# Storing the low halves of split projection weights once, and loading them in later groups

## The chip, the cores and the metric

The kernel runs on one core of one Trainium2 chip. The metric is the device time of one execution in microseconds; times of several executions are given as their median. The core has five engines that each work through a queue of their own in order: TensorE (PE, with its weight loads shown as PEld), VectorE (DVE), ScalarE (ACT), GpSimd (POOL) and SyncE (SP, which issues DMA transfers here; ACT and POOL issue some as well). An engine that waits for a semaphore holds back everything behind it in its queue.

## The reference

One layer of a residual block over 2048 tokens of width 1024, in float32. A normalised input goes through one wide projection, whose 5376 columns feed three consumers: chunk-band attention, an RWKV-7 recurrence, and two gates.

```python
h    = rms_norm(x, pre_mix_g)
proj = h @ w_in                       # (2048, 1024) @ (1024, 5376)
p_att, p_rwkv, p_gate = proj[:, :1536], proj[:, 1536:3328], proj[:, 3328:] + gate_bias
y_a  = chunk_band_attention(*split(p_att, 3), rel_bias)
y_b  = rwkv7_time_mix(p_rwkv, ...)
m    = sigmoid(gate_a) * (y_a @ proj_a) + sigmoid(gate_b) * (y_b @ proj_b)
x    = x + rms_norm(m @ w_out, post_mix_g)
x    = x + rms_norm(square(relu(rms_norm(x, pre_ffn_g) @ w_up)) @ w_down, post_ffn_g)
```

## The kernel before

The 2048 tokens are worked off in four groups of 512. Each group runs `phase_rwkv` (14 column blocks of the RWKV part, 16 of the gates, and the recurrence), `phase_attention` (12 column blocks, three for each of four head pairs: q, k, v) and `phase_merge` (the two branch projections and `w_out`, with the next group's normalisation beside them). The feed-forward part follows after all four groups.

A matmul in full float32 precision is made from three in a faster 32-bit format: every operand is split into a high part (a rounded copy) and a low part (what the rounding lost), and high times high, high times low and low times high are added up in PSUM. `split` (L80) makes the parts: ACT copies the high part (L81), DVE subtracts it from the raw values (L83). For weights, `wsplit` (L70) first has SP load the raw block of 128 by 1024 values, 512 KB (`load_raw`, L64), into a buffer `wraw`, and writes `whi` and `wlo`. Each of the three has two buffers, so the raw load for a block waits until the block two earlier has been split, and the parts of a block are written when the matmuls of the block two earlier have read theirs. The same buffers serve `proj_a`, `proj_b` and `w_out`.

`dense` (L118) makes one column block of 128 columns: it calls `wsplit` and then issues 24 matmuls of 128x512 (`mm3`, L86): eight of the high weight with the high input (`hh,whi` in the profile), eight of the high weight with the low input (`hl,whi`), and last the eight that read the low weight (`hh,wlo`). All 42 blocks (14 + 16 + 12) are made in each of the four groups, from the same weights, so each weight block is loaded and split four times. In the first group the first two blocks are loaded ahead (`self.raws`), and their low parts are made by POOL instead of DVE.

The order of each engine's queue comes from a scheduler that goes through the program with estimated times. Some places are fixed by hand: `queue_behind` puts one instruction behind another of the same engine, `follow` (L112) does it for the two split instructions of a block behind the instructions that emptied an earlier PSUM bank (`self.emptied`), and the constants `GATES`, `STEPS`, `BLOCKS`, `TURNED`, `FIFTH`, `BONUS`, `SCORES` and `TURNS` place small matmuls of the recurrence among the dense ones by number.

Other lines that are spoken of below: L399 and L400 (POOL copies the last column of a block for the token shift), L497 (POOL copies row scales `n`), L738 and L743 (matmul `ps_st` and DVE update `ST` of the recurrence), L713 and L716 (`TQ`), L770 to L784 (the recurrence's output, `yn`, stored as `yd` by POOL), L585 (`ps_A`), L926 and L927 (keys `KK` and values `VV` of the group before, loaded by SP), L960 and L961 (their stores by POOL), L988 to L1018 (attention scores `ps_s`, row minima `mn`, exponentials, `PT`, `ps_pv`), L1077 (the bias of a head, loaded by SP), L1149 (the branch projections, `th`), L1178 and L1189 (`ps_o`, `o`), L1200 and L1202 (the rows of the group before, loaded by SP for `residual`), L1231 and L1255 (`cmb`, `wd`: sums of `w_down` blocks, made beside the groups and moved by POOL).

Of the kernel before, what the change touches and what calls it, by code (L numbers as in the profile page):

```python
# [9 lines left out]
F32 = mybir.dt.float32  # L10
BF16 = mybir.dt.bfloat16
F32R = mybir.dt.float32r
# [4 lines left out]
DRAM = bass.MemoryType.DRAM  # L17

P = 128
D = 1024  # L20
KB = D // P
# [17 lines left out]
BONUS = {(0, 1): 138, (1, 0): 258}  # L39
SCORES = 150  # L40
TURNS = {1: (588, 592)}
DEC = math.exp(-0.5)

ATT0 = 0
# [12 lines left out]
class Block:  # L57
# [54 lines left out]
    def follow(self):  # L112

        for ins, done in zip((self.high.ins, self.low), self.emptied[-3] if len(self.emptied) > 2 else ()):
            if done is not None:
                self.queue_behind(ins, done.ins)

    def dense(self, col):  # L118

        first = bool(self.raws)  # L120
        wh, wl = self.wsplit(self.w_in(col), "w", KB, P, lower=self.nc.gpsimd if first else None)
        if first:
            n = 1 - len(self.raws)
            self.queue_behind(self.high.ins, self.highs[n])
        self.follow()
        ps = self.pd.tile([P, G], F32, tag="d", name="psd")
        terms = [(wh[:, k], wl[:, k], self.h[0][:, k], self.h[1][:, k]) for k in range(KB)]
        if first:
            pairs = [(u, h) for u, _, h, _ in terms] + [(v, h) for _, v, h, _ in terms] + [(u, l) for u, _, _, l in terms]
            self.mm = [  # L130
                self.nc.tensor.matmul(ps, l, r, start=n == 0, stop=n == len(pairs) - 1).ins
                for n, (l, r) in enumerate(pairs)
            ]
            self.queue_behind(self.mm[0], self.last_transpose)
        else:
            self.mm = self.mm3(ps, terms, True)
        self.dl += self.mm
        return ps
# [19 lines left out]
    def constants(self, ctx, mixing):  # L158
        tc, nc, a = self.tc, self.nc, self.a
        keep = ctx.enter_context(tc.tile_pool(name="const", bufs=1))  # L160
        cp = mixing.enter_context(tc.tile_pool(name="mconst", bufs=1, side="right"))
        dp = ctx.enter_context(tc.tile_pool(name="scratch", bufs=1, space=DRAM))
        nrow = sum(n for _, n in ROWS)
        self.cst = cp.tile([P, nrow], F32, name="cst")
        nc.sync.dma_start(self.cst, a["cst"])
# [279 lines left out]
    def rwkv_pre(self, g, p, rp, NA, between=lambda: None):  # L445
# [20 lines left out]
        between()  # L466
        nc.vector.tensor_scalar(tw, tw, -0.5 * DEC, -0.5 * DEC, ALU.mult, ALU.add)
        cum = tw
# [279 lines left out]
    def rwkv_post(self, p, R):  # L748
# [18 lines left out]
        for h in range(2):  # L767
            ps = self.pr.tile([C, 4, P], F32, tag="wus", name="ps_yt")
            for j in range(4):
                mm = nc.tensor.transpose(ps[:, j], yn[:, h * 4 + j], self.ident)  # L770
                if j == 0 and p in TURNS:
                    self.place(mm, TURNS[p][h])
            cs = slice(h * 4, h * 4 + 4)
# [876 lines left out]
```

## Time and profile before

| | |
|---|---|
| median of 3 executions | 3199.82 us (3198.31 to 3202.85) |
| profiled execution | 3198.07 us, of which the span from first to last instruction is 3196.4 us |
| PE busy | 3147.3 us, 98% of the span |
| DVE busy | 2235.8 us, 70% |
| ACT busy | 1578.7 us, 49% |
| POOL busy | 613.8 us, 19% |
| DMA | 598.82 MB, mean 187 GB/s |
| granted clock of TensorE | 0.999 |

How to read the profile's lines: a line of a group of instructions gives the kernel's line, the engine, the operation, output and inputs by the program's names, the shape, and the count after an x; behind the bar the busy time in us and the mean of one in ns; behind the second bar the idle time of the engine just before them and what ended most of it. A line of waits gives who waited, for whom, the total in us, how many times, and the longest. A line of the DMA issues gives the queue, the count, the size of one, and the median time from issue to landing. A line of the timeline gives start and length in us, the engine (SPq, POOLq: an engine's queue that waits or issues), the operation, and how many were merged. "issue" as a releaser means that the engine waited for nothing that the profile shows.

### The profile page before, as it was taken

Reading aid. Unit: us, or ns where it says so; the run is one execution under the profiler, and the core shown is the slowest. Engines: PE = TensorE matmul, PEld = TensorE weight load, DVE = VectorE, ACT = ScalarE, POOL = GpSimd, SP = SyncE. Lnnn points to the kernel's source line nnn. Section 1 sums busy time; section 2 is a strip of 40 time slices with the busy share of each in tenths; the row PEclk is TensorE's granted clock in tenths of the full one; section 3 lists DMA queues with packets and bytes.
Section 4 is the critical chain, followed back from the end, with each engine's and each line's share of the span. In section 5 each row is a group of like instructions: output and inputs, shape, how many; then the busy total and the mean of one; then the engine's idle time right before and its main releaser. Section 6 shows DMA issues by size and latency. Waiting matters only on the chain. (4 is left out here: it accounts for less than half of the span.)

```text
span 3196.4 us, 49803 instructions
## 1 busy us (share of the span) xinstructions
PE 3147.3 (98%) x18800; PEld 2575.3 (81%) x18800; DVE 2235.8 (70%) x3668; ACT 1578.7 (49%) x2511; POOL 613.8 (19%) x1119
## 2 busy tenths in 40 slices
PE   8999999999999999999999999999999999999998
PEld 6877788778888877888877888888888878888887
DVE  6785667776767786767876776877656768765564
ACT  5435645445745445745534755454544454444343
POOL 3222012132112222112222101221211112210000
PEclk9999999999999999999999999999999999999999
DMA  6245473157573246574236466554877866547565
GB/s 192 86 135 189 134 259 129 60 172 244 175 260 129 77 141 245 186 235 160 94 116 228 160 208 261 192 179 162 293 268 251 281 225 213 170 156 244 191 221 174
DMA packets 197477, 598.82 MB, mean 187 GB/s; under 512 B 25570, under 2 KB 25708, under 8 KB 197236
## 3 DMA queue, kind: packets, MB, share of 16 engines
q1 hardware_dynamic: 139124, 415.24, 40.1%
q0 software_dynamic: 48896, 163.61, 13.6%
q10 hardware_dynamic: 9216, 16.78, 1.4%
q8 instruction: 148, 2.42, 0.3%
q14 instruction: 93, 0.76, 0.1%
HBM read 431.67 MB, written 167.01 MB: 187 GB/s over the span
## 5 line engine op out<-in xcount | busy, mean ns | idle before, releaser
L1469 PE MATMUL ps_dn<-fop 128*128 128x512 f32 x2688 | 610.8, 389 | 0.0
L1469 PEld LDWEIGHTS ps_dn<-fop 128*128 128x128 f32 x2688 | 504.1, 188 | 104.7 <-DVE fop L83 0.2
L81 ACT CAST whi<-wraw 128x1024 fp32r<-128x1024 f32 x232 | 243.5, 1049 | 284.4 <-PE psd L92 202.5
L83 DVE TENSOR_TENSOR wlo<-wraw,whi 128x1024 fp32r<-128x1024 f32 x230 | 280.6, 1220 | 125.4 <-ACT whi L81 80.2
L92 PE MATMUL psd<-hh,whi 128*128 128x512 f32 x1328 | 357.9, 398 | 1.1 <-ACT k L401 1.0
L92 PE MATMUL psd<-hh,wlo 128*128 128x512 f32 x1328 | 356.8, 398 | 0.0
L92 PE MATMUL psd<-hl,whi 128*128 128x512 f32 x1328 | 354.3, 397 | 0.0
L92 PEld LDWEIGHTS psd<-hl,whi 128*128 128x128 f32 x1328 | 243.6, 188 | 47.9
L92 PEld LDWEIGHTS psd<-hh,wlo 128*128 128x128 f32 x1328 | 242.7, 188 | 48.3
L92 PEld LDWEIGHTS psd<-hh,whi 128*128 128x128 f32 x1328 | 241.2, 188 | 50.0 <-ACT k L401 1.6
L83 DVE TENSOR_TENSOR fop<-xraw,fop 128x1024 fp32r<-128x1024 f32 x112 | 137.0, 1223 | 176.2 <-ACT fop L81 175.8
L81 ACT CAST fop<-xraw 128x1024 fp32r<-128x1024 f32 x112 | 117.8, 1052 | 251.0 <-PE ps_dn L1469 191.9
L1339 POOL DMA_DIRECT2D xd<-X x192 | 104.1, 542 | 380.3 <-ACT X L1336 318.2
L83 DVE TENSOR_TENSOR fop<-wdraw,fop 128x1024 fp32r<-128x1024 f32 x112 | 136.6, 1219 | 19.7 <-ACT fop L81 19.4
L81 ACT CAST fop<-wdraw 128x1024 fp32r<-128x1024 f32 x112 | 117.6, 1050 | 35.7 <-DMA wdraw<-in_w_down_dram 22.7
L994 DVE CUSTOM_DVE_ANT_0 sc<-bias,ps_s 128x640 f32<-128x640 f32 (+4 forms) x128 | 93.8, 733 | 39.3 <-PE ps_s L988 23.3
L1012 DVE TENSOR_TENSOR PTl<-ps_pt,PTh 128x640 fp32r<-128x640 f32 (+4 forms) x128 | 94.3, 737 | 27.7 <-ACT PTh L1011 26.8
L1001 ACT ACTIVATE sc<-sc,mn 128x640 f32<-128x640 f32 (+4 forms) x128 | 97.8, 764 | 31.8 <-DVE mn L994 30.4
L81 ACT CAST s12h<-s 128x1024 fp32r<-128x1024 f32 x32 | 33.7, 1053 | 155.5 <-PE ps_u L92 155.5
L92 PE MATMUL ps_p<-yh,whi 128*128 128x512 f32 x256 | 101.7, 400 | 4.9 <-DVE th L1149 2.2
L92 PE MATMUL ps_p<-yl,whi 128*128 128x512 f32 x256 | 101.5, 397 | 0.3 <-DVE yl L83 0.2
L1178 PE MATMUL ps_o<-whi,mh 128*128 128x512 f32 x256 | 100.5, 392 | 0.7 <-DVE o L1189 0.6
(374 smaller groups left out, 6804.0 us busy)
## 6 DMA issues: line engine op xcount, KB each, us to landing
wraw<-in_w_in_dram SPq DMA_DIRECT2D x168, 512.0 KB, 3.7
xraw<-xd SPq DMA_DIRECT2D x112, 512.0 KB, 4.5
xd<-X POOLq DMA_DIRECT2D x192, 256.0 KB, 4.7
wraw<-in_w_up_dram SPq DMA_DIRECT2D x80, 512.0 KB, 4.4
wdraw<-wd SPq DMA_DIRECT2D x64, 512.0 KB, 4.8
wdraw<-in_w_down_dram SPq DMA_DIRECT2D x48, 512.0 KB, 5.0
gd<-gate ACTq DMA_DIRECT2D x64, 256.0 KB, 2.5
wd<-cmb POOLq DMA_DIRECT2D x64, 256.0 KB, 3.7
```

Of the source, the lines that this page charges most:

```text
L81: high = self.high = self.nc.scalar.copy(hi, src)
L83: self.low = lower.tensor_tensor(lo, src, hi.bitcast(F32), ALU.subtract).ins
L92: mm.append(nc.tensor.matmul(ps, l, r, start=n == 0, stop=n == last).ins)
L994: least = nc.vector.tensor_tensor_reduce(sc[:, 0:n], bias[:, s0:640], pss[:, c0 : c0 + n], 1.0, 3.0e38, ALU.add, ALU.min, mn,)
L1001: nc.scalar.activation(sc[:, 0:n], sc[:, 0:n], AF.Exp, scale=-1.0, bias=mn, accum_out=sm[:, col : col + 1])
L1012: nc.vector.tensor_tensor(lv, pst[:, 0:nk], hv.bitcast(F32), ALU.subtract)
L1178: nc.tensor.matmul(ps[t], l[:, k, ts], r[:, k % 2], start=k == 0 and j == 0, stop=k == KB - 1 and j == 2)
L1339: nc.gpsimd.dma_start(self.xd[q][i // 2][:, i % 2], src)
L1469: nc.tensor.matmul(ps, o[:, l, k, sl], o[:, r, k], start=start and n == 0, stop=stop and n == end)
```

## The change

In the first group, the low part of every block is made as before and is then also stored to a DRAM scratch tile of 512 KB of its own (`wlow`, 42 of them) by a DMA that POOL issues. In the other three groups, `dense` loads the raw block as before and has ACT make the high part as before, but there is no subtraction: SP loads the low part from DRAM straight into the `wlo` buffer. `follow` has then only the ACT copy to put behind something. `LOWS` lists the blocks by number; it holds all 42. The matmuls and their order in the program are the same.

```diff
+LOWS = range(42)
...
     def follow(self):
 
         for ins, done in zip((self.high.ins, self.low), self.emptied[-3] if len(self.emptied) > 2 else ()):
-            if done is not None:
+            if done is not None and ins is not None:
                 self.queue_behind(ins, done.ins)
 
     def dense(self, col):
 
         first = bool(self.raws)
-        wh, wl = self.wsplit(self.w_in(col), "w", KB, P, lower=self.nc.gpsimd if first else None)
+        kept = self.lows.get(col)
+        if kept is None:
+            wh, wl = self.wsplit(self.w_in(col), "w", KB, P, lower=self.nc.gpsimd if first else None)
+            if col in self.keep_lows:
+                kept = self.lows[col] = self.dp.tile([P, KB, P], F32, name=f"wlow{col // P}")
+                self.nc.gpsimd.dma_start(kept, wl.bitcast(F32))
+        else:
+            raw = self.load_raw(self.w_in(col), KB, P)
+            wh, wl = (self.wp.tile([P, KB, P], F32R, tag="w" + x, bufs=2, name="w" + n) for x, n in (("h", "hi"), ("l", "lo")))
+            self.high = self.nc.scalar.copy(wh, raw)
+            self.low = None
+            self.nc.sync.dma_start(wl.bitcast(F32), kept)
...
-        dp = ctx.enter_context(tc.tile_pool(name="scratch", bufs=1, space=DRAM))
+        dp = self.dp = ctx.enter_context(tc.tile_pool(name="scratch", bufs=1, space=DRAM))
+        self.lows = {}
+        self.keep_lows = {i * P for i in LOWS}
```

## The prediction

> **What bounds the kernel now.** I read the table by engine first, then five stretches: the four groups (one pass each over 512 tokens, cut where the dense blocks of the next begin) and the feed-forward part.
>
> ```profile
> span 3196.4 us, 49803 instructions
> PE 3147.3 (98%) x18800; PEld 2575.3 (81%) x18800; DVE 2235.8 (70%) x3668; ACT 1578.7 (49%) x2511; POOL 613.8 (19%) x1119
> ...
> 0.00:483.00 483.00, 462.22 (x3149) 368.06 (x3150) 342.82 (x698) 241.25 (x448) 102.39 (x189) 1.00 0.50 164
> 483.00:976.00 493.00, 487.17 (x3417) 398.64 (x3416) 358.90 (x660) 255.47 (x442) 110.40 (x200) 1.00 0.51 172
> 976.00:1469.00 493.00, 488.21 (x3419) 399.00 (x3418) 359.44 (x661) 256.28 (x445) 109.51 (x201) 1.00 0.51 172
> 1469.00:1963.00 494.00, 488.45 (x3422) 400.01 (x3421) 357.10 (x651) 252.55 (x434) 101.12 (x184) 1.00 0.49 165
> 1963.00:3196.40 1233.40, 1221.24 (x5398) 1009.60 (x5396) 817.54 (x1001) 573.12 (x745) 190.42 (x347) 1.00 0.64 218
> ```
>
> A stretch lists its length, then busy time and count of PE, PEld, DVE, ACT and POOL, the clock, the DMA share and GB/s. In groups 1 to 3 PE is busy 487.17 to 488.45 us of 493 or 494, at full clock; DVE about 359. Those groups are the ones that the change relieves, and together they leave PE 493 + 493 + 494 - 487.17 - 488.21 - 488.45 = 16.2 us idle. Since "busy" may hide small gaps (matmuls overlap), I then asked what PE and its weight loads wait for, in these groups alone (first group of rows PE, second PEld):
>
> ```profile
> PE ps_st L738 <- DVE ST L743: 3.2, 3, 1.1
> PE ps_s L988 <- DVE mn L994: 2.4, 4, 0.7
> PE ps_p L92 <- DVE th L1149: 1.6, 3, 0.7
> PE ps_s L723 <- DVE TQ L716: 1.3, 3, 0.5
> PE ps_g L92 <- DVE yn L761: 1.2, 3, 0.4
> ...
> PE ps_o L1178 <- DVE wlo L83: 0.5, 1, 0.5
> PE ps_o L1178 <- DVE o L1189: 0.3, 1, 0.3
> PE ps_a L428 <- DVE BR L603: 0.2, 1, 0.2
> ...
> PEld ps_st L738 <- DVE ST L743: 12.5, 24, 1.5
> ...
> PEld ps_s L988 <- DVE mn L994: 9.7, 30, 1.0
> PEld ps_A L585 <- issue: 8.8, 24, 0.4
> ```
>
> The reader is to see how little is lost to DVE. All of PE's idle time that DVE ends is 3.2 + 2.4 + 1.6 + 1.3 + 1.2 + 0.5 + 0.3 + 0.2 = 10.7 us, in three groups. The weight loads show more, but the row of ps_A waits for nothing and yet costs 8.8 / 24 = 0.37 us each time: that is the price of the switch itself. Above it, ST leaves 12.5 - 24 x 0.37 = 3.6 us and mn (9.7 / 30 = 0.32 each) nothing on the mean.
>
> **The change part by part.** First, what one block costs and when it is needed.
>
> ```profile
> L83 DVE TENSOR_TENSOR wlo<-wraw,whi 128x1024 fp32r<-128x1024 f32 x230 | 280.6, 1220 | 125.4 <-ACT whi L81 80.2 <-PE psd L92 37.6 <-issue 6.8
> L92 PEld LDWEIGHTS psd<-hh,wlo 128*128 128x128 f32 x1328 | 242.7, 188 | 48.3
> ...
> 1028.54 1.23 DVE L83 TENSOR_TENSOR wlo<-wraw,whi 128x1024 fp32r<-128x1024 f32 x1 [1.00 <-PE psd L92]
> 1028.75 2.01 PE L92 MATMUL psd<-hh,whi 128*128 128x512 f32 x8
> 1030.60 1.98 PE L92 MATMUL psd<-hl,whi 128*128 128x512 f32 x8
> 1032.42 1.98 PE L92 MATMUL psd<-hh,wlo 128*128 128x512 f32 x8
> 1034.23 1.98 PE L92 MATMUL psd<-hh,whi 128*128 128x512 f32 x8
> ...
> wraw<-in_w_in_dram SPq DMA_DIRECT2D x168, 512.0 KB, 3.7
> kc<-KK POOLq DMA_DIRECT2D x12, 512.0 KB, 3.8
> KK<-kc SPq DMA_DIRECT2D x12, 512.0 KB, 4.8
> VV<-vc SPq DMA_DIRECT2D x12, 512.0 KB, 6.5
> ...
> 761.65 0.74 POOL L960 DMA_DIRECT2D kc<-KK  x1 [6.76 <-DVE KK L945]
> ```
>
> Removed: 3 x 42 = 126 subtractions x 1.220 = 153.7 us of DVE, 51 us a group, so about 359 falls to 308 of 493. Kept: 126 high copies on ACT, all matmuls. What is hidden behind PE is worth nothing; on the path lie at most the 10.7 us above, and below nothing cannot be excluded, as the order of the queues may come out worse. DVE sheds 51 / 359 = 14%. The rows name ST, mn and TQ, chains of their own that go on taking their time, and only one names wlo (0.5 us). I take 3 us gained of 10.7, nearer to the low end for that reason.
>
> Added: 126 loads of 512 KB on SP's queue, 66 MB in about 1480 us, 45 GB/s on top of 165 to 172, when the feed-forward stretch shows 218 with PE as busy. Each load waits until the last matmul of two blocks earlier has left the buffer (two buffers). From then to the third part of its own block, which reads the low part first, PE has to do one whole block (1034.23 - 1028.75 = 5.48 us) and two thirds of another (1032.42 - 1028.75 = 3.67), 9.1 us, less some 0.2 by which matmuls overlap. The load takes 3.7 to 6.5 us by the rows, so 2.4 us are left at the worst of them: hidden. If the cover goes (a landing over 9 us), PE waits for the rest, with nothing to make it up. Behind a waiting load stands SP's queue: later raw weights, bias, keys and values. But this queue waits today as well, for the subtraction of the block two earlier, which itself starts only when PE has left that buffer:
>
> ```profile
> SPq L67 <- DVE wlo L83: 956.9, 172, 36.4
> ...
> SPq L1077 <- DMA yd<-yf: 16.2, 3, 5.8
> ```
>
> So the new wait ends some 1.2 us sooner than the old one, and the raw loads, released by the ACT copy now, start earlier. Zero for these, with one exception in the rivals.
>
> Added in group 0: 42 stores issued by POOL, 0.74 us each by the kc row, 31 us on an engine that is busy 102 of 483, and 22 MB in those 483 us, 46 GB/s on top of 164, again within the 218. POOL waits for each subtraction and holds back what comes after it in its queue (the carry column of the token shift, the row scales n, cmb and wd traffic). The buffer is held until the store lands: 0.74 + 3.8 = 4.5 us after the subtraction, while the block that reads it starts only at 1034.23 in the steady rows and holds the buffer for 5.5 us more, to about 1039.7, against 1029.8 + 4.5 = 1034.3 for the store: some 5.4 us to spare. For more than that POOL must be late, and its longest wait of this kind in group 0 shows that it can be:
>
> ```profile
> POOL pr L399 <- DVE k L402: 15.5, 3, 12.3
> ```
>
> A store behind all of the 12.3 us would hold the subtraction of two blocks later back by 12.3 - 5.4 = 6.9 us, and what follows on DVE with it; the low part itself has 9.1 - 1.2 = 7.9 us to spare, so PE would not yet wait for it. Bounds: 0, and 6.9 if the work behind it on DVE is what PE needs next; I take 0.5, since one such wait is in the row and the next longest must fit in 15.5 - 12.3 = 3.2 us. The first two blocks are split on POOL itself, after the last operation that PE's start waits for, so nothing there. The feed-forward part is untouched.
>
> Sum against the profiled execution (3198.07 us, 1.7 over its span and 1.75 under the median of 3199.82): -3 + 0.5 = -2.5. To this I add 2 us for the exception below at less than full size. On the median that is 3199.82 - 0.5 = 3199.3, **3199 us**: no difference. About 0.2% (6.4 us) is what a measurement of this kernel can tell from no change.
>
> **The rivals.** *Slower: the v block of the first head pair waits for its low part.* At the start of attention in groups 1 to 3 SP's queue carries keys, values, the former group's rows and biases at once:
>
> ```profile
> 748.22 0.62 POOL L784 DMA_DIRECT2D yd<-yf  x1 [3.87 <-DVE yf L783]
> 749.35 7.15 SPq L1077 DMA_DIRECT2D bias<-skew  x2
> 750.56 1.98 PE L92 MATMUL psd<-hh,wlo 128*128 128x512 f32 x8
> 756.54 0.88 SPq L926 DMA_DIRECT2D KK<-kc  x1
> 757.47 0.60 SPq L927 DMA_DIRECT2D VV<-vc  x1
> 758.17 1.48 SPq L67 DMA_DIRECT2D wraw<-in_w_in_dram  x2
> 761.77 1.98 PE L92 MATMUL psd<-hh,wlo 128*128 128x512 f32 x8
> ```
>
> The second bias load stands until 756.2 for the landing of yd (the row L1077 <- yd above: three times, up to 5.8 us). The low part of the v block is free to load at 750.56 + 1.98 = 752.5 and needed at 761.77. Queued ahead of that bias it lands by 752.5 + 6.5 = 759.0, hidden. Queued behind bias, KK and VV it is issued at 758.1, lands by 764.6, and PE loses 2.8 us a group, 8.5 in all; if it takes as long as yd does in this burst (issued at 748.2, landed by 756.1: 7.9), it lands at 766.0, and PE loses 4.2 a group, 12.7 in all. It decides from 3.2 us a group on (9.5 less the 3 gained is 6.5). Which one is queued first the trace doesn't show; for the bad order speaks that KK and VV stand ahead of the raw weight that waits for just this block. With 3 gained and 0.5 lost in group 0: 3206 to 3210, 3208 in the middle. The Trainium skill's page "DMA: Bandwidth & Descriptors" (Issuing engines are not separate DMA queues) has the transfers of all queues run on the same 16 engines and interleave, so that a low part in the burst would push yd's landing, and with it that bias, later still; the 7.9 us for 256 KB beside a median of 3.7 for 512 KB of raw weights agree.
>
> *Faster: DVE's relief reaches PE.* If all 10.7 us of DVE-ended idle and the 3.6 of the ST loads went, 3199.8 - 14.3 = 3185.5; with two thirds of it, 3190. For it: DVE is the busiest engine beside PE. Against it: only one of the waiting rows names the work that goes. A larger gain needs PE to have room that its busy time hides. Weight loads are busy 81%; were the other 19% open, all 51 us a group could go, 3 x 51 = 153, to 3046. Against that stands the pace of the steady rows: eight matmuls every 32.42 - 30.60 = 1.82 us, in which eight weight loads of 188 ns are busy 83%, so that 81% is nearly all there is; chance under 0.01. The Trainium skill's page "Perfetto Trace Analysis" (Identifying the Most-Contended Engine) calls matmul busy time a bad measure of headroom and reads it from LDWEIGHTS busy instead; the trace agrees that busy PE is not PE at its peak, but its 83% is the ceiling here.
>
> *POOL's queue in group 0* costs its 6.9 us, and nothing is gained elsewhere: 3199.8 + 6.9 = 3207. *The change does nothing it says:* excluded, since the 42 column blocks (12 + 14 + 16) are all in the set, and each is loaded a whole group after its store.
>
> **How the numbers follow.** No measurable change 0.52 (own range 3194 to 3206); the late v block beyond the bound 0.25; other delays beyond it 0.07; faster beyond it 0.16. The late v block at less than full size is in the first case. Range for 8 in 10: from 3190 (two thirds of the gain) to 3212 (the v block at its 12.7 us with next to nothing gained). Faster 0.16, same 0.52, slower 0.32.
>
> **What would show it.** DVE busy of groups 1 to 3 near 308 each; 104 of the 230 subtractions left on it; PE busy unchanged within 3 us; PE's waits for ST, mn and TQ as long as now; a new row of loads wlo from DRAM, 126 of 512 KB, and 42 stores. For the rival: PE rows waiting for the DMA of the low part, three times, near the start of attention. The prediction is wrong if PE idle in groups 1 to 3 falls by more than 8 us, if it rises by that, or if group 0 grows by over 5 us.

## The result, and the profile after

The changed kernel takes 3226.74 us (median of 4, 3222.72 to 3227.6) against 3199.07 us of the kernel before beside it: ratio 1.0083, interval 1.0065 to 1.01, that is 27.7 us slower. The forecast was 3199, its range 3190 to 3212. The profiled execution took 3225.96 us:

```profile
span 3224.3 us, 49980 instructions
...
PE 3158.8 (98%) x18800; PEld 2579.8 (80%) x18800; DVE 2098.4 (65%) x3542; ACT 1576.5 (49%) x2511; POOL 606.0 (19%) x1161
```

By stretches, cut again where each group's dense blocks begin, the last one shortly behind `w_out` of group 3 (columns as in the prediction):

```profile
0.00:486.00 486.00, 464.33 (x3150) 370.10 (x3151) 342.11 (x698) 241.66 (x449) 125.51 (x232) 1.00 0.63 211
486.00:986.00 500.00, 489.75 (x3417) 399.16 (x3417) 313.35 (x618) 254.98 (x443) 100.09 (x201) 1.00 0.62 214
986.00:1488.00 502.00, 491.46 (x3417) 400.33 (x3417) 312.96 (x618) 254.45 (x443) 99.71 (x201) 0.99 0.62 213
1488.00:1986.00 498.00, 490.01 (x3415) 398.89 (x3414) 311.50 (x609) 252.11 (x433) 88.69 (x182) 1.00 0.60 205
1986.00:3224.30 1238.30, 1223.21 (x5406) 1011.36 (x5405) 818.51 (x1003) 573.26 (x747) 192.00 (x349) 1.00 0.64 217
```

Group 0 grew by 3 us, groups 1 to 3 by 7, 9 and 6, the rest by 3. The end of group 3 is taken here at the last matmul of `w_out`, which ends at 1960.7 us before and at 1985.5 now. VectorE's busy time fell by some 46 us a group. The idle time of TensorE in groups 1 to 3 rose from 16.2 us to 500 + 502 + 498 - 489.75 - 491.46 - 490.01 = 28.8 us, and its busy time rose as well, by 11.5 us over the whole run, although it does the same matmuls. What TensorE waits for in groups 1 to 3 now:

```profile
PE psd L93 <- ACT gate L804: 6.0, 3, 2.0
PE ps_pt L1021 <- DVE PTl L1026: 4.3, 3, 1.8
PE ps_t L674 <- ACT Z L669: 3.6, 4, 1.5
PE ps_s L1002 <- DVE mn L1008: 3.6, 5, 0.9
PE ps_y L756 <- DVE ST L757: 3.4, 3, 1.1
```

The first two rows are not in the list of before, the third stood there with 0.6 us, and none of them is work that the change touches. The first recurs once a group at the same place. Here is ScalarE's queue there, and the matmul behind it, in the changed kernel:

```profile
694.97 1.25 ACT L651 COPY XT<-XD 32x512 f32<-32x512 f32 x2 [5.15 <-DVE XD L646]
696.23 0.56 ACT L788 ACTIVATE yf<-ps_yt,cst 64x256 f32<-64x256 f32 x1
696.81 0.56 ACT L791 ACTIVATE yf<-ps_yt,gbo,gwo 64x256 f32<-64x256 f32 x1
697.39 1.04 ACT L131 CAST whi<-wraw 128x1024 fp32r<-128x1024 f32 x1
698.34 0.68 ACT L804 ACTIVATE gate<-psd,hgb 128x512 f32<-128x512 f32 x1
...
699.08 2.11 PE L93 MATMUL psd<-hh,whi 128*128 128x512 f32 x8 [1.99 <-ACT gate L804]
```

and at the same work in the kernel before:

```profile
687.31 0.56 ACT L774 ACTIVATE yf<-ps_yt,cst 64x256 f32<-64x256 f32 x1
687.88 0.56 ACT L777 ACTIVATE yf<-ps_yt,gbo,gwo 64x256 f32<-64x256 f32 x1
688.47 0.69 ACT L790 ACTIVATE gate<-psd,hgb 128x512 f32<-128x512 f32 x1
...
691.49 1.98 PE L92 MATMUL psd<-hh,wlo 128*128 128x512 f32 x8
```

Before, the gate was taken out of its PSUM bank directly behind the outputs `yf`. Now two copies `XT` stand ahead of it and wait 5.15 us for VectorE, and TensorE, which needs the bank for the next block, waits 1.99 us. What makes the gate late here is its place in ScalarE's queue. The scheduler writes the queues from estimated times, and 126 instructions fewer on VectorE shift these: of the 16112 matmuls in the built program, 561 now follow another one than before; of ScalarE's 2351 instructions, 293.

### The profile page after: what moved, and what is told of

Read it like the earlier page. It is cut to its first block, busy times and chain, and to the rows that moved or that the text cites. A ratio compares the mean times of both kernels' runs of the same rounds, so it can differ in the third digit from the quotient of the medians.

```text
span 3224.3 us, 49980 instructions
## 1 busy us (share of the span) xinstructions
PE 3158.8 (98%) x18800; PEld 2579.8 (80%) x18800; DVE 2098.4 (65%) x3542; ACT 1576.5 (49%) x2511; POOL 606.0 (19%) x1161
## 5 line engine op out<-in xcount | busy, mean ns | idle before, releaser
L84 DVE TENSOR_TENSOR wlo<-wraw,whi 128x1024 fp32r<-128x1024 f32 x104 | 126.8, 1219 | 71.2 <-ACT whi L82 56.6
L84 DVE TENSOR_TENSOR fop<-wdraw,fop 128x1024 fp32r<-128x1024 f32 x112 | 136.6, 1219 | 15.4 <-ACT fop L82 15.0
L727 DVE TENSOR_TENSOR TQ<-ps_tq,id 128x256 f32<-128x256 f32 x32 | 13.6, 424 | 155.6 <-PE ps_tq L724 155.6
L1025 ACT CAST PTh<-ps_pt 128x640 fp32r<-128x640 f32 (+4 forms) x128 | 79.8, 623 | 66.5 <-PE ps_pt L1021 65.8
```

The lines of the kernel that those rows point to most:

```text
L84: self.low = lower.tensor_tensor(lo, src, hi.bitcast(F32), ALU.subtract).ins
L727: nc.vector.tensor_tensor(TQ[:, cs, 0], ps[:, :, 0], self.id64[:, None, :].to_broadcast((P, 4, C)), ALU.add)
L1025: nc.scalar.copy(hv, pst[:, 0:nk])
```

## The experiments

Theories. *Order*: the queues came out worse. *Transfers*: the stores and loads hold others up. *Relief*: what the freed VectorE gives by itself. Differences below are medians against the kernel before in the same set of runs, in us; ratios carry 95% intervals. Line numbers of these kernels lie up to 40 higher than those of the kernel before.

**One part at a time.** Stores only: `dense` takes the splitting branch in every group and stores in the first one. Relief only: no store, no load, and a resident tile as low weight:

```diff
-            self.nc.sync.dma_start(wl.bitcast(F32), kept)
+            wl = self.h[1][:, :, 0:P]
```

> Group 0 stores the 42 low blocks as in the changed kernel, but groups 1 to 3 subtract as before and load no low block. The order of the instructions on TensorE, ScalarE, VectorE and SP is that of the kernel before, exactly. Order theory (the loss of groups 1 to 3 comes from the new order of the queues): only group 0 grows, by the 2.9 us seen at 248 to 254 us of the changed kernel, so about 3202 against 3199. Transfer theory, of the stores: the same 3202. Both put groups 1 to 3 back at 493 to 494 us each. If group 0 does not grow here, its 2.9 us were not of the stores.

> No store and no load of low blocks; groups 1 to 3 leave the subtraction out and the matmuls take a resident tile (a part of the low half of h) as the low weight, so the product differs from the reference there; time of TensorE is the same. DVE is freed as in the changed kernel, with none of its transfers. Order theory: the queues come out much as in the changed kernel (nearly the same order on TensorE and ScalarE), so 3215 to 3226, that is slower than 3199 by 16 us or more, with half-clock stretches after the long idles. Transfer theory: without the transfers the freed VectorE can only help, 3185 to 3199.

Stores only: 3203.64, +4.6 (1.0018, 1.0008 to 1.0027). Relief only: 3215.62, **+16.6** (1.0053, 1.0038 to 1.0068), although it does nothing but leave work out. The transfer theory alone falls. The row that the changed kernel had shows again, first among TensorE's waits of the relief alone:

```profile
PE psd L93 <- ACT gate L802: 6.1, 3, 2.0
```

A part of the stores' cost in the changed kernel is seen in group 0, where the order of TensorE, ScalarE and VectorE did not change (VectorE, then TensorE):

```profile
249.34 0.69 DVE L1245 TENSOR_TENSOR cmb<-cmb 128x512 f32<-128x512 f32 x1 [9.73 <-DMA cmb<-in_w_down_dram]
249.95 0.42 DVE L727 TENSOR_TENSOR TQ<-ps_tq,id 128x256 f32<-128x256 f32 x1
...
250.84 1.98 PE L737 MATMUL ps_s<-SV,BR 128*64 128x64 f32 x32 [2.41 <-DVE TQ L730]
```

Two stores issued at 237.3 and 241.2 run while a block of `w_down` is on its way; VectorE waits 9.73 us for it (8.3 before), `TQ` stands behind, and TensorE waits 2.41 us (0.9 before). The prediction looked at POOL's queue. That queue issued this load only 0.8 us later than before (240.62 against 239.86), but it landed after 8.7 us instead of 7.4: this wait came through the DMA engines. It explains some 1.5 of the 4.6 us. The profiled run of the stores alone shows the same wait (2.50 us), but it was the fastest of its ten (3200.94), and where the other runs lose the rest stays open.

**Order held.** The order of an engine's queue in one kernel is written down as positions in the program and given to the other:

```diff
+    def pin(self):
+        for engine, order in ORDER.items():
+            traced = [...]   # this engine's instructions in the program, but those in self.apart
+            for one, two in zip(order, order[1:]):
+                self.queue_behind(traced[two], traced[one])
```

In `apart` stand the instructions that only one of the two kernels has; the scheduler places them.

> The changed kernel, all its stores and loads in place, with the queues of TensorE and ScalarE held instruction by instruction to the order they have in the kernel before (the order is written down as a list and given to the scheduler). Order theory: groups 1 to 3 go back to 493 us each or a little below, group 0 keeps its 2.9 us, in all 3196 to 3204. Transfer theory: as the changed kernel, 3220 to 3230.

> The kernel before, no store and no load of low blocks and all subtractions in place, with the queues of all engines held to the order they have in the changed kernel (the 126 subtractions are left to the scheduler to place). Order theory: slower than before by most of the 24 us that groups 1 to 3 lost, so 3215 to 3235. Transfer theory: 3196 to 3203, as before.

> As the relief alone (no store, no load; groups 1 to 3 leave the subtraction out and take a resident tile as the low weight, so the product differs there), with the queues of TensorE and ScalarE held to the order of the kernel before. The relief alone in its own order took 3215.6. If the order of these two queues made that loss: 3192 to 3200. If it was made by the order of VectorE or of SP, which are left free here: 3208 to 3218.

The changed kernel in the order of before on two engines: 3220.18, +21.2 (1.0065, 1.005 to 1.008). The order theory had said 3196 to 3204: a miss. The kernel before, meant to run in the order of after: 3214.90, +15.9 (1.0051, 1.0036 to 1.0066), about what this theory said. But the run is not the test that its expectation describes. Its `ORDER` lists POOL's queue alone; TensorE, ScalarE and SP kept the order of the kernel before, and the rows for `ST` and `mn` are those of before (3.2 and 2.4 us). Its largest row is not in the changed kernel's list:

```profile
PE ps_s L748 <- DVE TQ L741: 11.6, 3, 4.4
```

It comes from POOL (here in group 1):

```profile
700.86 1.63 POOL L664 COPY XT<-XD 32x512 f32<-32x512 f32 x2 [23.86 <-DVE XD L657]
702.44 0.54 POOL L1280 DMA_DIRECT2D cmb<-in_w_down_dram  x1
...
715.88 0.69 DVE L1256 TENSOR_TENSOR cmb<-cmb 128x512 f32<-128x512 f32 x1 [9.97 <-DMA cmb<-in_w_down_dram]
718.67 1.15 PE L748 MATMUL ps_s<-SV,BR 128*64 128x64 f32 x32 [3.10 <-DVE TQ L741]
```

POOL's two copies `XT` stand far ahead of their place before and wait 23.86 us (10.08 before). Seven loads of `w_down` blocks stand behind them, where it was three. VectorE waits at `cmb` for a landing (9.97 us, 7.85 before), `TQ` stands behind, and TensorE waits for it. So the order of one engine that is busy 19% of the span can cost 15.9 us. TensorE's list of the changed kernel has no row for `TQ` in groups 1 to 3, so the 15.9 us are no measure of what the order cost there.

The relief alone in the order of before on two engines: 3201.74, +4.4 (1.0013, 1.0004 to 1.0022): 12.2 better than in its own order, but no gain. By the starts of the dense blocks it gained 3 us up to the end of the recurrence of group 1 and lost nearly 4 in the attention, where TensorE waited more for `mn` and `PTl` of VectorE, whose order was free. So VectorE was held as well, and with it SP and POOL. For that the four subtractions of a combination `cmb` had to be untied: the program ties each to the VectorE instruction written before it, six times a low part that is gone now.

> The relief alone once more (no store, no load, groups 1 to 3 leave the subtraction out and take a resident tile as the low weight, so the product differs there), now with all five queues in the order of the kernel before, the four subtractions of a combination on VectorE among them, which the program ties to the VectorE instruction written before them (often a subtraction that is gone now). Under the order of TensorE and ScalarE alone, the recurrence gained some 2.5 us a group and the attention gave 3.5 back. If the order of VectorE gave it back: 3189 to 3194. If the freed VectorE is worth nothing in any order: 3197 to 3203.

> The changed kernel, its 42 stores and 126 loads put in by the scheduler, everything else on all five queues in the order of the kernel before. If order is all of the loss beside the stores: 3193 to 3200 (the relief, and 4.6 for the stores). If the loads cost by themselves: over 3203, up to the 3210 that their cost in the order of TensorE and ScalarE (some 14) would give.

Relief with all five queues in the order of before: **3190.38, -7.4** (0.9975, 0.9966 to 0.9984). The same work left out costs 16.6 us in the order that the scheduler writes and gains 7.4 in the old one. Which of the three queues added here gained the last 11.8 us is not told apart. The changed kernel with all five held: 3211.38, **+13.6** (1.0042, 1.0029 to 1.0054). Order alone is thus not all: 21.0 us lie between these two, and 4.6 are the stores.

**Where the loads cost.** First attempts:

> The changed kernel in the order of the kernel before on TensorE and ScalarE (3220.2 so far), and on SP's queue the load of a low block stands behind the raw load that the program makes next, where so far it stood ahead of it and held it up while it waited for its own buffer. If what was left came from raw loads held up on SP's queue: 3203 to 3211. If it came from the load on the DMA engines or from the order of VectorE: 3217 to 3223.

> The changed kernel (3226.7) with the same turn on SP's queue and all else left to the scheduler. If raw loads held up on SP's queue carry a part of the loss: 3212 to 3221, and the half-clock stretches that follow a late cast go. If not: 3224 to 3229.

> Stores as in the changed kernel, and in groups 1 to 3 the same 126 blocks of 512 KB read from DRAM, but copied to another place in DRAM, where nobody waits for them (no room for them in SBUF); the subtractions stay, and TensorE, ScalarE and VectorE keep the order of the kernel before. So the load on the DMA engines is there, without a wait for a buffer and without relief or a new order. If the load on the DMA engines makes the loss: 3214 to 3222. If it is the waits on SP's queue and the orders: the 3203.6 of the stores alone, and up to 3 us more.

The load of a low block behind the next raw load changed nothing in the order of before (3220.18, +22.8; 1.0078, 1.0063 to 1.0093) and gained in its own order (3217.39, +20.0; 1.0066, 1.0051 to 1.0081), where the other queues moved too, so that it can't be told what gained. The transfers alone took 3244.35 (1.0151, 1.0134 to 1.0168) and missed their aim: no instruction held the copies back, and all 126 ran in the first group, as the stretches say (DMA share and GB/s at the end):

```profile
0.00:500.00 500.00, 455.96 (x3059) 362.11 (x3060) 326.94 (x676) 231.03 (x431) 123.81 (x227) 0.97 0.92 332
500.00:1000.00 500.00, 495.08 (x3453) 405.15 (x3452) 362.89 (x664) 257.75 (x445) 111.35 (x202) 1.00 0.51 171
```

Group 1 began only at 519.8 us (482.8 before). At 332 GB/s a raw weight block landed after 9.0 us in the median of the first 500 us; in the changed kernel, at 211 GB/s, after 4.4, and before after 3.7.

> Transfers alone, put right: the copies of the run before them had all been issued in the first group, and are now each queued behind the raw load of their own block. Stores as in the changed kernel, the 126 copies of 512 KB go to another place in DRAM, nobody waits for them, subtractions stay, and all queues keep the order of the kernel before. If the load on the DMA engines in groups 1 to 3 makes a loss: 3208 to 3220. If the loss comes only where a queue waits for a low block's own buffer: 3203 to 3206.

Paced, the transfers alone took 3224.44, +26.7 (1.0086, 1.0072 to 1.01), above the 3208 to 3220 that the theory of the DMA engines had. So transfers can cost that much with subtractions, order and buffers as before; they were copies from DRAM to DRAM, of another shape, so the size is not that of the loads.

With all five queues held, one can see where the loads cost: between the relief and the changed kernel the starts of the blocks of group 1 move apart by 2.0, 0.8 and 4.3 us at the 33rd, 35th and 36th block and nowhere else by 0.4; in group 2 by 1.5, 1.0 and 5.3 and in group 3 by 1.8, 0.8 and 1.4 at the same blocks. These are among the six blocks of the first two head pairs, at the start of the attention. SP's queue there, for the relief:

```profile
741.30 0.33 SPq L79 DMA_DIRECT2D wraw<-in_w_in_dram  x1
742.12 0.58 SPq L964 DMA_DIRECT2D KK<-kc  x1
742.87 0.48 SPq L965 DMA_DIRECT2D VV<-vc  x1
743.89 0.32 SPq L1238 DMA_DIRECT2D o_prev<-od  x1
744.25 0.64 SPq L1240 DMA_DIRECT2D xr<-in_x_dram  x1
```

and with the loads:

```profile
743.40 0.40 SPq L79 DMA_DIRECT2D wraw<-in_w_in_dram  x1
751.63 0.32 SPq L159 DMA_DIRECT2D wlo<-wlow  x1
752.12 0.58 SPq L966 DMA_DIRECT2D KK<-kc  x1
752.86 0.48 SPq L967 DMA_DIRECT2D VV<-vc  x1
753.39 0.42 SPq L1240 DMA_DIRECT2D o_prev<-od  x1
753.86 0.45 SPq L1242 DMA_DIRECT2D xr<-in_x_dram  x1
```

The load of a low block stands ahead of `KK` and waits until 751.63 for its buffer. Keys, values and the former group's rows are issued 10 us later (2 us of this is the lead that the relief has here, 741.30 against 743.40). The next raw load, behind one more low block that waits, is issued at 760.00 instead of 754.77. TensorE's largest waits in groups 1 to 3 are then these:

```profile
PE ps_pt L1047 <- DVE VV L998: 5.2, 2, 2.6
PE ps_s L1028 <- DMA KK<-kc: 4.6, 3, 1.7
```

The first is a chain over ScalarE and VectorE: two casts wait for their raw blocks, a part of `VV` stands behind the second one, and VectorE waits for it:

```profile
771.88 1.05 ACT L157 CAST whi<-wraw 128x1024 fp32r<-128x1024 f32 x1 [2.50 <-DMA wraw<-in_w_in_dram]
...
774.47 1.04 ACT L157 CAST whi<-wraw 128x1024 fp32r<-128x1024 f32 x1 [1.38 <-DMA wraw<-in_w_in_dram]
775.42 0.26 ACT L997 CAST VV<-ps_vt 128x128 fp32r<-128x128 f32 x1
...
775.71 0.29 DVE L998 TENSOR_TENSOR VV<-ps_vt,VV 128x128 fp32r<-128x128 f32 x1 [2.30 <-ACT VV L997]
...
776.06 1.26 PE L1047 MATMUL ps_pt<-ident,sc 128*128 128x128 f32 x5 [2.58 <-DVE VV L998]
```

The next runs change `LOWS` alone, all five queues held:

```diff
-LOWS = range(42)
+LOWS = range(12, 42)                                  # recurrence and gates
+LOWS = (0, 1, 4, 5, 8, 9)                             # the six blocks
+LOWS = all but (0, 1, 4, 5, 8, 9, 39, 40)             # 39, 40: the stores at 237 and 241 us
```

> As the run before it, with the low parts of the 30 blocks of recurrence and gates alone stored and loaded; the 12 blocks of attention are split in every group, as before. The late transfers were seen at the start of the attention, where the loads of low blocks stand among KK, VV, the residual and the bias. If the loads cost there: 3190 to 3198, faster than the changed kernel in any order. If they cost evenly: a third of their cost is gone and no more.

> Low parts of six blocks alone are stored and loaded, those of query, key and value of the first two head pairs (blocks 88 to 93 of the second group); all queues otherwise in the order of the kernel before. Place theory (the loads cost at these six blocks): most of the 16 us come with 18 of the 126 loads, 3208 to 3214. If the cost is spread over the loads: a seventh of it, 3198 to 3203.

> The other way round: the low parts of all blocks but these six, and but the two whose stores were late in the burst at 237 to 250 us of the first group, in the order of the kernel before. Place theory: relief without the two losses, 3190 to 3195, faster than the kernel before by 4 to 9 us. If the cost of the loads moves on to the next blocks of the attention: 3200 or more.

> The same 34 blocks with no order held: the changed kernel with a shorter list and nothing else. Order theory: some 15 us above the run in the order of before, 3204 to 3212. If the losses at the six blocks and in the first group were what made the changed kernel slower: 3190 to 3200.

Without the attention's blocks: 3196.03, -1.8 (0.9994, 0.9985 to 1.0004), 15.4 less than with them. The six blocks alone: 3212.68, **+13.9** (1.0046, 1.0033 to 1.0058), so 18 of the 126 loads bring nearly the whole cost. All but eight: 3195.54, **-3.3** (0.9989, 0.998 to 0.9998). The same 34 blocks in the scheduler's own order: 3215.03, **+16.2** (1.0051, 1.0038 to 1.0063), with the row of the gate back. It is above the 3204 to 3212 that the order theory had, so the order cost more than it said. This is still its plainest showing: one program, two orders, 19.5 us.

Is it SP's queue or the bytes? The loads of the low blocks go to POOL's queue, first all, then those of the six blocks:

```diff
-            self.nc.sync.dma_start(wl.bitcast(F32), kept)
+            queue = self.nc.gpsimd if col // P in SIX else self.nc.sync
+            queue.dma_start(wl.bitcast(F32), kept)
```

> All 42 blocks in the order of the kernel before (3211.4 so far), with the loads of the low blocks issued by POOL instead of SP. The DMA engines carry the same bytes, and SP's queue waits for no buffer of a low block. If SP's queue made the loss at the attention: 3195 to 3201. If the DMA engines made it: 3207 to 3215. POOL's own small operations then stand behind the loads, which could cost too and would show as ScalarE or TensorE waiting for POOL.

> Low parts of the six blocks alone, as in the run that took 3212.7, with their 18 loads issued by POOL. Same bytes at nearly the same time, and nothing of it in SP's queue. If SP's queue made the loss of 13.9 us: 3198 to 3203. If the bytes on the DMA engines made it: 3209 to 3214.

> 40 blocks (all but the two whose stores were late in the first group), the six blocks' loads on POOL's queue, the others on SP's, in the order of the kernel before. If SP's queue made the loss at the six blocks: 3191 to 3197, as the 34 blocks (3195.5) or a little better. If the bytes did: 3205 to 3211.

All loads on POOL: 3227.10, +28.3 (1.0083, 1.007 to 1.0097), inconclusive, since a low part stood behind POOL's own stores and brought a new wait once a group:

```profile
PE psd L104 <- DMA wlo<-wlow: 19.1, 3, 8.9
```

The six blocks on POOL: 3204.78, +7.3 (1.0022, 1.0012 to 1.0031), against 13.9 on SP. The two intervals do not meet: about half of the cost goes with the place in SP's queue. The trace agrees: TensorE's wait for `KK` is no longer among its largest, and the one for `VV` falls from 6.1 us to 2.8. The time is above the 3198 to 3203 expected of SP's queue alone; the rest may be the bytes in the burst. Forty blocks, the six of them on POOL: 3195.90, -1.6 (0.9995, 0.9986 to 1.0004), where the bytes theory had 3205 to 3211. The runs do not add up here: six blocks on POOL (+7.3) and the 34 others (-3.3) would make +4.0. What the remaining 7 us of the six blocks are, and why they do not show beside the others, stays open.

No version that does the whole computation is faster by over 0.2%. The best is the one with 34 blocks in the held order, by 0.11%.

## Why the prediction was wrong

By its own terms, each against the run that measured it:

| term | predicted | measured | from |
|---|---|---|---|
| relief of VectorE | -3 | -7.4 | relief, all queues held |
| stores in group 0 | +0.5 | +4.6 | stores only |
| loads on SP's queue, with the v block | +2 | +16.4 | 13.6 + 7.4 - 4.6 |
| order of the queues | 0 | +14.1 | 27.7 - 13.6 |

The last two rows are differences of runs, so that the sum is 27.7 by construction; apart from that, order was measured at 19.5 (34 blocks) and 24.0 (relief), and the loads at 13.9 (six blocks). These overlap, and the 14.1 is what is left of the order's loss where the loads cost too.

**Failed: "as the order of the queues may come out worse".** The prediction named it and gave it no price. It is one of the two largest terms. Only some places are fixed by hand; the rest follows the scheduler, and taking 126 instructions out of one queue wrote the queues of the other engines anew.

**Failed: "the new wait ends some 1.2 us sooner than the old one".** No run measured the 1.2 us; outside the first two head pairs the loads cost nothing that shows (34 blocks: -3.3). What counts is what stands behind the wait. In the kernel before the first `KK` is issued at 746.67, and in the prediction's own rows the next one at 756.54, ahead of the raw loads of 758.17; the low load that waits for its buffer was put ahead of the first `KK`. The rival of the late v block had the right place, the first blocks of the attention, and the right burst, but the wrong victim: TensorE waited hardly at all for a low part (0.2 us in the changed kernel), but for keys, values and raw weights queued behind one.

**Mis-sized: the stores.** 0.5 came from POOL's queue; 4.6 was measured. The two stores in the burst of 237 to 250 us pushed the landing of a `w_down` block, and `TQ` stood behind its consumer on VectorE. This part, some 1.5 us, went over a transfer whose landing the prediction had not priced; the rest is open.

**Mis-sized: the relief.** The bound of 14.3 holds; the 3 within it should have been 7.4, half. One of the eight waiting rows named the subtraction; that it also stands ahead of the others' work in VectorE's queue is the likely reason for more, and no run shows it.

**Right:** VectorE fell to 311.5 to 313.4 us a group (308 said), 104 subtractions are left, 126 loads and 42 stores appear, and no engine became the bound:

```profile
L84 DVE TENSOR_TENSOR wlo<-wraw,whi 128x1024 fp32r<-128x1024 f32 x104 | 126.8, 1219 | 71.2 <-ACT whi L82 56.6
...
wlo<-wlow SPq DMA_DIRECT2D x126, 512.0 KB, 4.8
...
wlow<-wlo POOLq DMA_DIRECT2D x42, 512.0 KB, 5.5
```

The landing of 4.8 us in the median is within the 3.7 to 6.5 assumed, but between 740 and 800 us, at the start of the attention, the median of seven low loads was 7.9. **Wrong signs:** TensorE's busy time was to stay within 3 us and rose by 11.5; its idle time in groups 1 to 3 rose by 12.6, beyond the 8 that were to prove the prediction wrong.

## What to carry to other kernels

Where a scheduler writes the queues, a change that takes instructions out of one engine also changes the order of the others; compare the orders before trusting a sum of terms, and measure the change once in the old order, since that alone tells what the removed work was worth. Compare the seldom busy engines too: POOL's order alone cost 15.9 us here. A wait in a queue is priced by what stands behind it at that place, not by its mean length: look where the queue carries other loads in a burst. With TensorE busy for 98% of the span, taking work from a neighbour that is busy 70% gained 0.25% at best here, and order and loads can each cost more than that.

## What the runs showed of the hardware

Half clock followed short idle stretches of TensorE. The changed kernel has five such spells in its body (at 251, 711, 1199, 1213 and 1701 us), the kernel before none until its last 10 us. One of them, after the wait for the gate of group 2 (stretches with the columns of before: the clock is the third number from the right; then a line of the timeline):

```profile
1197.00:1199.40 2.40, 0.42 (x3) 0.35 (x3) 1.38 (x2) 1.93 (x3) 1.69 (x5) 1.00 0.50 178
1199.42:1202.82 3.40, 3.40 (x10) 2.62 (x9) 0.00 (x0) 1.62 (x2) 2.61 (x5) 0.50 0.82 167
1202.90:1206.00 3.10, 3.10 (x73) 2.43 (x73) 0.00 (x0) 0.00 (x0) 0.00 (x0) 1.00 0.95 357
...
1199.01 3.46 PE L93 MATMUL psd<-hh,whi 128*128 128x512 f32 x8 [1.98 <-ACT gate L804]
```

After 1.98 us without a matmul the clock is 0.50 for 3.4 us, and eight matmuls take 3.46 us instead of 2.0. Five spells of 3.41 us, 17 us at half clock, are 8.5 us of lost work by this estimate, out of the 11.5 by which the busy time rose. Over all profiles but that of the transfers alone with their full first group, between 30 and 3150 us, a spell followed on 4 of 129 idle stretches of 1.0 to 1.8 us, on 18 of 35 of 1.8 to 2.8 us, and on 10 of 11 longer ones. No run took the spells away alone, so the 8.5 us are a reading and not an experiment. By the profiles they lie mainly in the terms of order and loads: there are five spells for the relief in its own order and three for the changed kernel with all queues held, but none for the relief with all queues held. The spell at 251 follows the wait that the stores made; the profile of the stores alone has none. The Trainium skill's page "TensorE: Matmul & The Clock Gate" (What's actually happening) has half rate set in after an idle window of about 3.4 us, windows that run freely; the length of a spell agrees, but here idle stretches of about 2 us were enough in half of the cases.
